# Other scratch tiles for the quadrant sums, and an earlier place for the next layer's value weights, in a two-layer encoder kernel

## The chip, the cores and the metric

The kernel runs on one core of a Trainium2 chip. The metric is the device time of one execution in microseconds (us), given as the median of several runs. The engines are called as in the profile: PE (TensorE, with PEld for its weight loads), DVE (VectorE), ACT (ScalarE), POOL (GpSimd) and SP (SyncE, whose queue issues all the DMAs here). Each engine runs its own instructions in the order in which they stand in the program.

## The reference

Two layers over 512 tokens of width 1024, in float32. What matters here is the end of a layer and the start of the next one:

```
for l in range(2):
    proj = x @ w_in[l]                       # 1024 x 6816; columns 1024..1535 are the values of neighbourhood attention
    ... three attentions, gates, merge ...
    x = layer_norm(ALPHA * x + merged @ w_out[l])
    gu = x @ w_ffn_in[l]                     # 1024 x 5632
    hidden = silu(gu[:, :2816]) * gu[:, 2816:]
    x = layer_norm(ALPHA * x + hidden @ w_ffn_out[l])
```

## The kernel before, in words

Every float32 operand is split into a high and a low part (`split`, `wsplit`: ACT copies the high part with a rounding, L138 or L221; DVE subtracts it for the low part, L139 or L222), and each product is three matmuls (high x high, high x low, low x high). `x` is kept transposed as `xth` and `xtl`. A scheduler fixes the order of the instructions on every engine when the program is built; the order of the code, the buffers of the pools and the slots decide what it may move.

**Feed-forward.** The 2816 hidden columns are 11 sets of 256. `CHUNKS` groups the sets in four chunks of 3, 3, 3 and 2. The first set of a layer is `ffn_plain`. The others are `ffn_fast`, a Strassen-like scheme on quadrants of `x` (two halves of the 1024 rows by two halves of the tokens) with seven products instead of eight. PE's seven products (L778) go into three PSUM tiles: `px` and `pz` (both of tag `sc`) and `py` (tag `pv`). `py` takes three products one after the other (sum t2, sum t3, sum t4), and DVE reads it between them (L844, L848, L857), so that the next product waits for that read. Two buffers each serve `sc` and `pv`.

**The quadrant sums.** The sums of quadrants of `x` (t1 to t4) are made once in each layer, in its first fast set, by `x_sums` (L731 to L760): for each of two halves nine DVE adds and subtractions of 128x512, and four splits (four ACT copies L221, four DVE subtractions L222). Its three scratch tiles come from the pool tag `P` (`ptile`, four buffers). The same four buffers hold the plain set's two `hidden` tiles (`sg`, L784 and L785) and the fast set's `p1`. The 16 slots of the sums stay taken until after the last set.

**Slots.** `R` is a first-in first-out list of 38 tiles of 128x512 (names r0_74 and so on in the rows). The list is worked through while the program is built, so the place of a `put` in the code decides which tiles the next `get` receives.

**The down products.** `ffn_down` loads weights of `w_ffn_out` in pieces of 512 KB into the two `raw` buffers, splits them, and adds each token tile's product to `xt` on DVE (L878). The down product of a chunk is put behind the first two sets of the next chunk, one half of the columns behind each. The last chunk's down product stands at the end of the layer. Ahead of it, in layer 0, `wload_slots` loads the value weights of layer 1 (four pieces of 512 KB through the same two `raw` buffers) and splits them into 16 slots of `R`. A `raw` buffer is free for its next load when both halves of the piece in it have been split.

Of the kernel before, what the change touches and what calls it, by code (L numbers as in the profile page):

```python
# [9 lines left out]
F32 = mybir.dt.float32  # L10
# [8 lines left out]
DEPTH = 2  # L19
D_IN = 6816  # L20
D_FF = 2816
# [5 lines left out]
C_NQ, C_NK, C_NV = 0, 512, 1024  # L27
# [54 lines left out]
def trunk(ctx, tc, x, ln_in, w_in, feat, bias, lamv, w_mla, w_mlr, w_mlv, w_branch, w_out,  # L82
# [36 lines left out]
    def ptile():  # L119
        return dp.tile([128, 512], F32, tag="P", name="P", bufs=4)  # L120
# [76 lines left out]
    def wload_slots(src_of, ncol, steps):  # L197

        res, slots, k = [], [], 0
        for n in steps:  # L200
            raw = wp.tile([128, 1024], F32, tag="raw", name="raw", bufs=2)
            rv = raw[:, :n * ncol].rearrange("p (k c) -> p k c", k=n)
            c = 0
            for src in src_of(k * 128, (k + n) * 128):
                w = src.shape[1]
                nc.sync.dma_start(rv[:, :, c:c + w], src.rearrange("(k p) c -> p k c", p=128))
                c += w
            hl = ([], [])
            for a in range(0, n * ncol, 512):
                hi, lo = R.get(), R.get()  # L210
                split(hi, lo, raw[:, a:a + 512])
                hl[0].append(hi)
                hl[1].append(lo)
            slots += hl[0] + hl[1]
            res.append((k, n, tuple(Pairs(i, ncol) for i in hl)))
            k += n
        return res, slots
# [66 lines left out]
    na_v, na_slots = [], []  # L284
# [447 lines left out]
    def x_sums():  # L732

        h = lambda kh, th: f32(quad(xth, kh, th))
        lo = lambda kh, th: f32(quad(xtl, kh, th))
        two = lambda t: t.rearrange("p (k c) -> p k c", k=2)
        res = [[], [], [], []]
        for i in range(2):
            ts = [ptile() for _ in range(3)]
            t1, t2, d = (two(t) for t in ts)  # L740
            q = lambda a: a[:, 2 * i:2 * i + 2]

            def halves(n, t):
                hl = (R.get(), R.get())
                split(*hl, t)
                res[n].append(hl)

            V.tensor_sub(t1, q(h(0, 1)), q(h(0, 0)))
            V.tensor_sub(d, q(lo(0, 1)), q(lo(0, 0)))
            V.tensor_add(t1, t1, d)  # L750
            V.tensor_sub(t2, q(h(1, 1)), t1)
            V.tensor_add(t2, t2, q(lo(1, 1)))
            halves(1, ts[1])
            halves(0, ts[0])
            V.tensor_sub(d, t2, q(h(0, 0)))
            V.tensor_sub(d, d, q(lo(0, 0)))
            halves(2, ts[2])
            V.tensor_sub(t1, q(h(1, 0)), t2)
            V.tensor_add(t1, t1, q(lo(1, 0)))
            halves(3, ts[0])  # L760
        return res
# [51 lines left out]
    def ffn_fast(l, m, sums):  # L813


        early = not sums

        def load(t, base, kh):
            c = slice(base + m * 128, base + (m + 2) * 128)
            nc.sync.dma_start(t.rearrange("p (k c) -> p k c", k=4),  # L820
                              w_ffn_in[l, kh * 512:(kh + 1) * 512, c].rearrange("(k p) c -> p k c", p=128))
            return t

        def halved(t, now=True):
            return wsplit(t, 1024, now)

        g0, u0, u1 = load(H.get(), 0, 0), load(H.get(), D_FF, 0), load(H.get(), D_FF, 1)
        s = H.get()
        g1 = load(wp.tile([128, 1024], F32, tag="raw", name="raw", bufs=2), 0, 1)
        px, py, pz = bank("sc"), bank("pv"), bank("sc")  # L830
        product(px, halved(g0, not early), from_x(0, 0), True)
        p1 = ptile()
        A.activation(p1, px, AF.Copy)  # L833
        if early:
            product(px, halved(g1, False), from_x(1, 0), False)
            sums += x_sums()
        t1, t2, t3, t4 = sums
        with tc.high_priority():
            V.tensor_add(s, u0, u1)
            V.tensor_sub(u0, g0, u0)  # L840
            V.tensor_sub(g0, s, g0)
        product(py, halved(g0), from_sum(t2), True)
        u2 = ptile()
        V.tensor_add(u2, py, p1)  # L844
        product(pz, halved(s), from_sum(t1), True)
        product(py, halved(u0), from_sum(t3), False)
        u3 = ptile()
        V.tensor_add(u3, py, p1)  # L848
        V.tensor_add(u3, pz, u3)
        if not early:  # L850
            product(px, halved(g1), from_x(1, 0), False)
        with tc.high_priority():
            V.tensor_sub(g1, g1, g0)
        product(pz, halved(g1), from_x(1, 1), False)
        V.tensor_add(u2, pz, u2)
        product(py, halved(u1), from_sum(t4), False)
        V.tensor_add(p1, py, p1)  # L857
        H.put(s, u0, g0, u1)
        res = [hidden(px, p1)]
        res.append(hidden(u2, u3))  # L860
        return res

    def ffn_down(l, m0, sets, xt, first, hfs):

        n = 2 * len(sets)
        act = tuple(HidTiles(sets, i) for i in range(2))
        chs = []
        for hf in hfs:
            c = slice(hf * 512, (hf + 1) * 512)
            chs.append((c, wload_ks(lambda a, e: [w_ffn_out[l, m0 * 128 + a:m0 * 128 + e, c]], 512, (2,) * (n // 2))))  # L870
        for t in range(NT):
            for c, ch in chs:
                p = bank("acc")
                gemm_x(p, ch, slice(0, 512), act, tsl(t), n)
                if first:
                    V.scalar_tensor_tensor(xt[t][:, c], xt[t][:, c], ALPHA, p, op0=OP.mult, op1=OP.add)
                else:
                    V.tensor_add(xt[t][:, c], xt[t][:, c], p)  # L878
            yield t
        if 1 in hfs:  # L880
            for st in sets:
                for hl in st:
                    R.put(*hl)


    for l in range(DEPTH):
# [87 lines left out]
        for c, (m0, n) in enumerate(CHUNKS):  # L974
            sets = []
            for i in range(n):
                m = 2 * (m0 + i)
                if m0 + i == 0:
                    sets.append(ffn_plain(*plain[0]))
                else:  # L980
                    sets.append(ffn_fast(l, m, sums))
                if done is not None and i < 2:
                    for _ in ffn_down(l, *done, xt, c == 1, (i,)):
                        pass
            done = 2 * m0, sets
        for t in sums:
            for hl in t:
                R.put(*hl)
        gb = load_gb(ln2[l])
        if l < DEPTH - 1:  # L990
            na_v, na_slots = wload_slots(lambda a, e: [w_in[l + 1, a:e, C_NV:C_NV + 512]], 512, (2, 2, 2, 2))
        for t in ffn_down(l, *done, xt, False, (0, 1)):
            layer_norm(xt[t], *gb)
            if l == DEPTH - 1:
# [93 lines left out]
```

## Time and profile before

| | |
|---|---|
| median of 3 runs | 1885.93 us (1885.37 to 1889.29) |
| the profiled execution's own time | 1881.28 us |
| its span, first to last instruction | 1879.3 us |
| PE busy | 1822.4 us, 97% of the span |
| DVE busy | 1331.0 us, 71% |
| ACT busy | 906.0 us, 48% |
| mean granted TensorE clock | 0.990 |

The span is what the trace covers, and the execution's own time is 2 us longer. PE leaves 57 us of the span idle. A matmul that is issued late, or that runs at the half clock, counts as busy for longer, so the busy share alone does not tell what could be saved.

### The profile page before, as it was taken

How to read it: one execution, taken by the hardware profiler on the slowest of the kernel's cores; microseconds unless marked ns; L12 is line 12 of the kernel's file. 1: busy time of each engine (PE TensorE's matmuls, PEld its weight loads, DVE VectorE, ACT ScalarE, POOL GpSimd, SP SyncE). 2: the span in 40 equal slices, each digit the busy share in tenths (PEclk: the TensorE clock that was granted, in tenths of full speed). 3: DMA queues.
4: the chain of work that ended last, by engine and by line, in shares of the span. 5: the costliest groups of instructions: out<-in, count | busy, mean ns of one | idle time of the engine just before them, and what ended most of it. 6: DMA issues, size and time to landing. Idle time of an engine off the chain costs nothing.

```text
span 1879.3 us, 28551 instructions
## 1 busy us (share of the span) xinstructions
PE 1822.4 (97%) x11200; PEld 1623.1 (86%) x11200; DVE 1331.0 (71%) x2228; ACT 906.0 (48%) x1620; POOL 87.8 (5%) x165
## 2 busy tenths in 40 slices
PE   7999999999998899999899999999999979999998
PEld 6988899988878899999689888999888779899996
DVE  6488886666567877777556888866656678777766
ACT  3567776555423443333326677755554234343431
POOL 4100000000000000000001000000000000000001
PEclk9999999999999899999999999999999999999999
DMA  7453232223251232323345432322233412323332
GB/s 256 120 156 101 89 87 77 79 79 96 90 191 46 68 113 86 117 87 105 126 132 150 127 96 86 91 62 85 74 107 122 147 57 68 115 92 114 96 102 78
DMA packets 167765, 195.86 MB, mean 104 GB/s; under 512 B 8528, under 2 KB 132688, under 8 KB 167632
## 3 DMA queue, kind: packets, MB, share of 16 engines
q1 hardware_dynamic: 167632, 194.05, 33.1%
q8 instruction: 88, 1.44, 0.3%
q14 instruction: 45, 0.37, 0.1%
HBM read 177.24 MB, written 9.44 MB: 99 GB/s over the span
## 4 chain that ended last, share of the span: by engine, by line
PE 89%; DVE 5%; DMA 3%; ACT 2%; issue 1%; SPq 0%; POOLq 0%; DVEq 0%; POOL 0%; ACTq 0%
PE acc L156 18%; PE acc L157 18%; PE acc L158 18%; PE sc L778 10%; PE pv L778 8%; DVE wlo L139 2%; PE tr L648 2%; PE pv L491 1%; DMA raw<-in_w_ffn_in_dram 1%; PE pv L656 1%; PE pv L655 1%; PE sc L477 1%; PE sc L632 1%; PE sc L631 1%; PE sc L476 1%
## 5 line engine op out<-in xcount | busy, mean ns | idle before, releaser
L139 DVE TENSOR_TENSOR wlo<-raw,whi 128x1024 fp32r<-128x1024 f32 (+4 forms) x242 | 287.9, 1191 | 127.1 <-ACT whi L138 124.1
L138 ACT ACTIVATE whi<-raw 128x1024 fp32r<-128x1024 f32 (+4 forms) x242 | 249.9, 1033 | 253.3 <-PE acc L157 49.4
L138 ACT ACTIVATE whi<-f 128x1024 fp32r<-128x1024 f32 x100 | 104.6, 1056 | 214.2 <-PE acc L158 118.8
L156 PE MATMUL acc<-whi,r 128*128 128x512 f32 (+1 forms) x504 | 195.6, 394 | 9.7 <-ACT whi L138 6.1
L156 PE MATMUL acc<-xth,whi 128*128 128x512 f32 x512 | 204.0, 398 | 0.6 <-ACT f L672 0.6
L158 PE MATMUL acc<-xth,wlo 128*128 128x512 f32 x512 | 202.7, 396 | 0.0
L157 PE MATMUL acc<-xtl,whi 128*128 128x512 f32 x512 | 202.6, 396 | 0.0
L157 PE MATMUL acc<-wlo,r 128*128 128x512 f32 (+1 forms) x504 | 198.5, 394 | 1.1 <-DVE wlo L139 1.1
L158 PE MATMUL acc<-whi,r 128*128 128x512 f32 (+1 forms) x504 | 197.7, 392 | 0.0
L778 PE MATMUL pv<-r,whi 128*128 128x256 f32 x960 | 176.0, 282 | 8.8 <-DVE P L844 3.1
L156 PE MATMUL acc<-whi,xth 128*128 128x256 f32 (+2 forms) x544 | 161.8, 299 | 1.6 <-ACT whi L138 1.6
L157 PE MATMUL acc<-wlo,xth 128*128 128x256 f32 (+2 forms) x544 | 162.4, 299 | 0.8 <-DVE wlo L139 0.8
L158 PE MATMUL acc<-whi,xtl 128*128 128x256 f32 (+2 forms) x544 | 162.4, 299 | 0.0
L778 PEld LDWEIGHTS pv<-r,whi 128*128 128x128 f32 x960 | 148.6, 189 | 12.1 <-DVE P L844 3.5
L139 DVE TENSOR_TENSOR wlo<-f,whi 128x1024 fp32r<-128x1024 f32 x100 | 121.5, 1221 | 29.7 <-ACT whi L138 25.8
L778 PE MATMUL sc<-xth,whi 128*128 128x256 f32 x480 | 134.3, 280 | 3.9 <-ACT P L833 3.9
L778 PE MATMUL pv<-r,wlo 128*128 128x256 f32 x480 | 134.7, 281 | 0.0
L778 PE MATMUL sc<-xtl,whi 128*128 128x256 f32 x480 | 133.8, 279 | 0.0
L778 PE MATMUL sc<-xth,wlo 128*128 128x256 f32 x480 | 133.5, 279 | 0.0
L156 PEld LDWEIGHTS acc<-whi,r 128*128 128x128 f32 x504 | 94.8, 190 | 32.3 <-ACT whi L138 6.8
L157 PEld LDWEIGHTS acc<-wlo,r 128*128 128x128 f32 x504 | 95.4, 189 | 23.0 <-DVE wlo L139 2.7
L158 PEld LDWEIGHTS acc<-whi,r 128*128 128x128 f32 x504 | 95.7, 190 | 21.1
(231 smaller groups left out, 4296.1 us busy)
## 6 DMA issues: line engine op xcount, KB each, us to landing
raw<-in_w_in_dram SPq DMA_DIRECT2D x64, 512.0 KB, 3.6
f<-in_w_ffn_in_dram SPq DMA_DIRECT2D x60, 512.0 KB, 3.5
raw<-in_w_ffn_out_dram SPq DMA_DIRECT2D x44, 512.0 KB, 3.6
raw<-in_w_in_dram SPq DMA_DIRECT2D x64, 256.0 KB, 3.3
raw<-in_w_ffn_in_dram SPq DMA_DIRECT2D x28, 512.0 KB, 3.6
raw<-in_w_branch_dram SPq DMA_DIRECT2D x24, 512.0 KB, 3.4
raw<-in_w_out_dram SPq DMA_DIRECT2D x16, 512.0 KB, 3.6
r<-r SPq DMA_DIRECT2D x56, 128.0 KB, 2.5
```

Of the source, the lines that this page charges most:

```text
L138: A.activation(hi[:, :n], raw[:, :n], AF.Copy)
L139: V.tensor_sub(lo[:, :n], raw[:, :n], f32(hi[:, :n]))
L156: T.matmul(o, lh[0], rh[0], start=first, stop=False)
L157: T.matmul(o, lh[0], rh[1], start=False, stop=False)
L158: T.matmul(o, lh[1], rh[0], start=False, stop=last)
L476: T.matmul(sc, qs[j][:, tsl(t)], ks[j][0], start=True, stop=False)
L477: T.matmul(sc, qs[j][:, tsl(t)], ks[j][1], start=False, stop=True)
L491: T.matmul(po[:, 0:256], ch_[:, tsl(k)], v, start=k == 0, stop=False)
L631: T.matmul(sc, q[0][:, tsl(t)], k[0], start=True, stop=False)
L632: T.matmul(sc, q[0][:, tsl(t)], k[1], start=False, stop=False)
L648: T.transpose(pt[:, tsl(i)], prs[i % 2][:, tsl(kp + i // 2)], ident)
L778: T.matmul(o[:, c], w[a][:, j, f], x[e], start=fresh and mi == 0 and j == 0 and n == 0, stop=j == 3 and n == 2, skip_group_check=True)
```

## The change

Three edits. In `x_sums` the three scratch tiles are no longer three of the four `P` tiles: two are taken from the gates' tag `gt` (two buffers) and one from the tag `o32` (one buffer, here named `xs`), both of which the attention phase used before. The sums' slots are returned to `R` right behind the last set, ahead of the down product that follows it. And the value weights of layer 1 are loaded while that down product (the third chunk's second half) is built, behind its first token tile, instead of after it.

```diff
--- before.py
+++ after.py
@@ -736,7 +736,7 @@
         two = lambda t: t.rearrange("p (k c) -> p k c", k=2)
         res = [[], [], [], []]
         for i in range(2):
-            ts = [ptile() for _ in range(3)]
+            ts = gate_tiles() + [dp.tile([128, 512], F32, tag="o32", name="xs", bufs=1)]
             t1, t2, d = (two(t) for t in ts)
             q = lambda a: a[:, 2 * i:2 * i + 2]
 
@@ -979,16 +979,18 @@
                     sets.append(ffn_plain(*plain[0]))
                 else:
                     sets.append(ffn_fast(l, m, sums))
+                last = m0 + i == D_FF // 256 - 1
+                if last:
+                    for t in sums:
+                        for hl in t:
+                            R.put(*hl)
                 if done is not None and i < 2:
-                    for _ in ffn_down(l, *done, xt, c == 1, (i,)):
-                        pass
+                    for t in ffn_down(l, *done, xt, c == 1, (i,)):
+                        if last and t == 0 and l < DEPTH - 1:
+                            na_v, na_slots = wload_slots(lambda a, e: [w_in[l + 1, a:e, C_NV:C_NV + 512]],
+                                                         512, (2, 2, 2, 2))
             done = 2 * m0, sets
-        for t in sums:
-            for hl in t:
-                R.put(*hl)
         gb = load_gb(ln2[l])
-        if l < DEPTH - 1:
-            na_v, na_slots = wload_slots(lambda a, e: [w_in[l + 1, a:e, C_NV:C_NV + 512]], 512, (2, 2, 2, 2))
         for t in ffn_down(l, *done, xt, False, (0, 1)):
             layer_norm(xt[t], *gb)
             if l == DEPTH - 1:
```

What this does to the order on three engines follows. **DVE, layer 0, where the plain set ends and the first fast set starts, before** (xth and xtl are the transposed `x`, f tiles hold raw weights, P_5813 and P_5914 are the plain set's two `sg`, L748 to L759 are the sums' adds):

```order
L841 TENSOR_TENSOR f1_113<-f2_114,f1_113 128x1024
L222 TENSOR_TENSOR xtl_73<-tr_5706,xth_72 128x4x128
L853 TENSOR_TENSOR raw_5922<-raw_5922,f1_113 128x1024
L139 TENSOR_TENSOR wlo_6029<-f1_113,whi_6028 128x1024
L785 TENSOR_TENSOR P_5813<-P_5813,pv_5715 128x512
L139 TENSOR_TENSOR wlo_6059<-f2_114,whi_6058 128x1024
L222 TENSOR_TENSOR r3_77<-P_5813,r2_76 128x512
L785 TENSOR_TENSOR P_5914<-P_5914,pv_5716 128x512
L222 TENSOR_TENSOR r31_105<-P_5914,r30_104 128x512
L748 TENSOR_TENSOR P_5985<-xth_72 128x512
L749 TENSOR_TENSOR P_5987<-xtl_73 128x512
L139 TENSOR_TENSOR wlo_6087<-f0_112,whi_6086 128x1024
```

**The same twelve places after the change:**

```order
L748 TENSOR_TENSOR gt_5985<-xth_72 128x512
L841 TENSOR_TENSOR f1_113<-f2_114,f1_113 128x1024
L222 TENSOR_TENSOR xtl_73<-tr_5706,xth_72 128x4x128
L749 TENSOR_TENSOR xs_5987<-xtl_73 128x512
L853 TENSOR_TENSOR raw_5922<-raw_5922,f1_113 128x1024
L785 TENSOR_TENSOR P_5813<-P_5813,pv_5715 128x512
L139 TENSOR_TENSOR wlo_6029<-f1_113,whi_6028 128x1024
L750 TENSOR_TENSOR gt_5985<-gt_5985,xs_5987 128x512
L139 TENSOR_TENSOR wlo_6059<-f2_114,whi_6058 128x1024
L222 TENSOR_TENSOR r3_77<-P_5813,r2_76 128x512
L751 TENSOR_TENSOR gt_5986<-xth_72,gt_5985 128x512
L222 TENSOR_TENSOR r20_94<-gt_5985,r12_86 128x512
```

All nine adds of the first half, two of its splits and the second half's first add (twelve instructions) now stand ahead of L785 on P_5914, the multiplication that waits for the plain set's last product and that comes eight rows behind the ones shown; before, all of them stood behind it. In layer 1 the same rows move in the same way.

**PE, layer 0, the first fast set, before** (pv_5925 is `py`; w..6086 are the weights of the product with t3, w..6147 those with t4, and w..6194 those of the next set's first product):

```order
L778 MATMUL pv_5925<-r23_97,whi_6086 128x256
L778 MATMUL pv_5925<-r5_79,whi_6086 128x256
L778 MATMUL pv_5925<-r23_97,wlo_6087 128x256
L778 MATMUL sc_6191<-xth_72,whi_6194 128x256
L778 MATMUL sc_6191<-xtl_73,whi_6194 128x256
L778 MATMUL sc_6191<-xth_72,wlo_6195 128x256
L778 MATMUL sc_6191<-xth_72,whi_6194 128x256
```

**After:**

```order
L778 MATMUL pv_5925<-r23_97,whi_6086 128x256
L778 MATMUL pv_5925<-r5_79,whi_6086 128x256
L778 MATMUL pv_5925<-r23_97,wlo_6087 128x256
L778 MATMUL pv_5925<-r14_88,whi_6147 128x256
L778 MATMUL pv_5925<-r16_90,whi_6147 128x256
L778 MATMUL pv_5925<-r14_88,wlo_6148 128x256
L778 MATMUL pv_5925<-r14_88,whi_6147 128x256
```

Before, 23 matmuls of the next set's first product stood between the product with t3 and that with t4; now the product with t4 follows at once, and the next set's product stands behind the first set's last one.

**DVE at the end of layer 0, before** (raw_8819, 8825, 8831 and 8837 are the four pieces of the value weights, acc_8737 to acc_8797 the four token tiles of the third chunk's down product, raw_8843 and the following ones the weights of the last down product, lam1 a scalar of layer 1):

```order
L222 TENSOR_TENSOR r6_80<-raw_8825,r8_82 128x512
L902 TENSOR_TENSOR lam1_9084<-ring_126 128x1
L878 TENSOR_TENSOR f3_115<-f3_115,acc_8737 128x512
L903 TENSOR_SCALAR lam1_9084<-lam1_9084 128x1
L878 TENSOR_TENSOR f5_117<-f5_117,acc_8757 128x512
L222 TENSOR_TENSOR r28_102<-raw_8831,r0_74 128x512
L878 TENSOR_TENSOR f6_118<-f6_118,acc_8777 128x512
L222 TENSOR_TENSOR r25_99<-raw_8825,r27_101 128x512
L222 TENSOR_TENSOR r7_81<-raw_8831,r9_83 128x512
L878 TENSOR_TENSOR f4_116<-f4_116,acc_8797 128x512
L222 TENSOR_TENSOR r29_103<-raw_8837,r1_75 128x512
L222 TENSOR_TENSOR r20_94<-raw_8837,r12_86 128x512
```

**After** (raw_8757, 8763, 8769 and 8775 are now the pieces of the value weights):

```order
L222 TENSOR_TENSOR r21_95<-raw_8763,r13_87 128x512
L222 TENSOR_TENSOR r11_85<-raw_8763,r10_84 128x512
L222 TENSOR_TENSOR r35_109<-P_8714,r33_107 128x512
L878 TENSOR_TENSOR f3_115<-f3_115,acc_8737 128x512
L898 SCALAR_TENSOR_TENSOR P_9075,ring_126<-P_9075 128x64 x2
L222 TENSOR_TENSOR r24_98<-raw_8769,r26_100 128x512
L222 TENSOR_TENSOR r4_78<-raw_8769,r22_96 128x512
L878 TENSOR_TENSOR f5_117<-f5_117,acc_8781 128x512
L902 TENSOR_TENSOR lam1_9084<-ring_126 128x1
L222 TENSOR_TENSOR r5_79<-raw_8775,r23_97 128x512
L903 TENSOR_SCALAR lam1_9084<-lam1_9084 128x1
L222 TENSOR_TENSOR r16_90<-raw_8775,r14_88 128x512
```

The splits of the value weights now write other slots (the former sums' r13, r10, r26, r22, r23, r14 in place of r8, r0, r27, r9, r1 of the third chunk's hidden tiles), and all stand ahead of the third token tile's addition, which is the row behind these; the second and third L878 each stand behind a split of a piece that was loaded late. On SP one row moves: the third piece's load stands ahead of the load of layer 1's lambda vectors instead of behind it. Beyond these places, the orders are the same up to the names of slots.

## Rows read from the trace of the kernel before

**Rows 1.** The page, part 1: busy us, share of the span and instructions.

```profile
PE 1822.4 (97%) x11200; PEld 1623.1 (86%) x11200; DVE 1331.0 (71%) x2228; ACT 906.0 (48%) x1620; POOL 87.8 (5%) x165
```

**Rows 2.** Stretches: length, busy per engine (instructions), PEclk, DMA share, GB/s.

```profile
599.74:636.25 36.51, 26.67 (x195) 25.28 (x194) 30.85 (x41) 13.84 (x19) 0.00 (x0) 0.86 0.09 29
612.00:618.00 6.00, 2.29 (x9) 1.93 (x9) 5.90 (x10) 1.71 (x3) 0.00 (x0) 0.50 0.15 53
1534.10:1569.55 35.45, 26.75 (x195) 25.36 (x194) 29.66 (x41) 12.76 (x18) 0.00 (x0) 0.86 0.10 31
915.95:942.59 26.64, 20.04 (x73) 14.89 (x73) 17.63 (x25) 5.38 (x6) 2.50 (x4) 0.87 0.46 155
```

**Rows 3.** Timeline of DVE, layer 0: start, us, line, operation, idle before and its releaser.

```profile
583.27 1.23 DVE L839 TENSOR_TENSOR f<-f,f 128x1024 f32<-128x1024 f32 x1 [2.41 <-DMA f<-in_w_ffn_in_dram]
...
592.01 0.68 DVE L222 TENSOR_TENSOR r<-P,r 128x512 fp32r<-128x512 f32 x1
...
600.01 0.69 DVE L785 TENSOR_TENSOR P<-P,pv 128x512 f32<-128x512 f32 x1 [7.31 <-PE pv L158]
...
602.00 0.69 DVE L748 TENSOR_TENSOR P<-xth 128x512 f32<-128x512 f32 x1
...
603.69 1.22 DVE L139 TENSOR_TENSOR wlo<-f,whi 128x1024 fp32r<-128x1024 f32 x1 [0.40 <-ACT whi L138]
...
620.14 1.29 DVE L222 TENSOR_TENSOR r<-P,r 128x512 fp32r<-128x512 f32 x2
```

**Rows 4.** Timeline of PE, layer 0, the first fast sets.

```profile
604.20 0.39 PE L778 MATMUL sc<-xth,whi 128*128 128x256 f32 x1 [1.58 <-ACT P L833]
...
608.91 0.38 PE L778 MATMUL pv<-r,whi 128*128 128x256 f32 x1 [0.90 <-ACT r L221]
...
610.63 0.58 PE L778 MATMUL pv<-r,whi 128*128 128x256 f32 x1 [1.34 <-DVE r L222]
...
615.63 1.31 PE L778 MATMUL sc<-r,whi 128*128 128x256 f32 x2 [3.56 <-ACT r L221]
...
624.83 0.50 PE L778 MATMUL pv<-r,whi 128*128 128x256 f32 x2 [2.31 <-DVE P L844]
...
636.25 0.40 PE L778 MATMUL pv<-r,whi 128*128 128x256 f32 x2
...
645.74 0.40 PE L778 MATMUL pv<-r,whi 128*128 128x256 f32 x2
...
648.57 0.28 PE L778 MATMUL sc<-xth,whi 128*128 128x256 f32 x1
```

**Rows 5.** The page, part 6: loads by size, median us from issue to landing.

```profile
raw<-in_w_in_dram SPq DMA_DIRECT2D x64, 512.0 KB, 3.6
```

**Rows 6.** Timeline of ACT at the end of layer 0.

```profile
899.29 0.63 ACT L221 ACTIVATE r<-raw 128x512 fp32r<-128x512 f32 x1 [0.86 <-DMA raw<-in_w_in_dram]
...
912.96 0.63 ACT L221 ACTIVATE r<-raw 128x512 fp32r<-128x512 f32 x1 [5.39 <-PE acc L157]
...
917.92 1.15 ACT L221 ACTIVATE r<-raw 128x512 fp32r<-128x512 f32 x2 [2.93 <-DMA raw<-in_w_in_dram]
...
920.38 1.06 ACT L138 ACTIVATE whi<-raw 128x1024 fp32r<-128x1024 f32 x1 [1.31 <-DMA raw<-in_w_ffn_out_dram]
```

**Rows 7.** Timeline of SP's DMA queue at the end of layer 0: start, us until the last was issued.

```profile
894.70 5.61 SPq L206 DMA_DIRECT2D raw<-in_w_in_dram  x2
...
903.43 11.28 SPq L206 DMA_DIRECT2D raw<-in_w_in_dram  x2
...
915.74 10.52 SPq L129 DMA_DIRECT2D raw<-in_w_ffn_out_dram  x4
```

**Rows 8.** Timeline of PE at the end of layer 0, the two down products.

```profile
907.29 0.51 PE L156 MATMUL acc<-whi,r 128*128 128x512 f32 x1 [0.84 <-DVE lam L903]
...
921.49 0.80 PE L156 MATMUL acc<-whi,r 128*128 128x512 f32 x1 [5.54 <-ACT whi L138]
...
928.72 0.50 PE L157 MATMUL acc<-wlo,r 128*128 128x512 f32 x1 [0.35 <-DVE wlo L139]
```

## The prediction, made before the changed kernel ran

> **What bounds the kernel now.** I read the page's first part, then the waits of PE, then stretches of the places that the change touches, and last the timelines of each engine there. PE is busy for 97% of the span [rows 1], so it is the bound nearly everywhere, and a change helps only where PE stands still or runs slowly. Three such places lie where the change acts.
>
> The first two are the first fast set of each layer. I cut the stretch from the start of that set's first product to the start of the product with w6227 (192 matmuls of 128x256). It takes 36.51 us in layer 0 and 35.45 us in layer 1 [rows 2]. At full speed 24 such matmuls take 2.83 us (645.74 to 648.57 in [rows 4]), so 192 need 22.7. The excess, 13.8 and 12.8 us, has two parts. PE waits: 1.58, 0.90, 1.34, 3.56 and 2.31 us, 9.7 in all, mostly for the quadrant sums' splits, the last for L844 [rows 4]. And the granted clock is 0.86 over the stretch, 0.50 from 612 to 618 [rows 2]: the lower of its two levels, 1.2 GHz, after the waits had come close together. DVE tells why the sums are late. It works without a break once the adds begin at 602.00 and ends the last split at 621.4 (620.14 and 1.29), and just before, it stood still for 7.31 us in front of L785, which waited for the plain set's last product [rows 3]. The sums need only `xth` and `xtl`, which DVE had finished before 592.01 [rows 3].
>
> The third place is the end of layer 0. PE ends the third chunk's down product at 915.95 and waits 5.54 us for the last down product's first weights, then three short ones behind it (the last, 0.35, in [rows 8]). From 915.95 to 942.59 the clock is 0.87 [rows 2]. The chain backward: that weight piece's load was issued at 915.74 [rows 7] and split from 920.38 [rows 6]. It waited for a `raw` buffer, the buffer for a split of value weights, and that split stood still for 5.39 us until 912.96 for PE's L157 on acc [rows 6]: it writes a slot that the third chunk's down product was still reading.
>
> **The change part by part.** No instruction is added or removed; the sum is all in order and waits. Durations: a DVE operation of 512 columns 0.69 us, followed by the next after 0.60; the low split of 1024 columns 1.22, next after 1.13 [rows 3]; an ACT copy of 512 0.63, of 1024 1.06 [rows 6].
>
> *Scratch tiles, DVE.* Twelve instructions of the sums move ahead of that L785. From L839 at 583.27 [rows 3] I walk the new order. L748 starts at 586.3; the first half's adds, in between the set's other work, run until 599.5; L748 of the second half ends 600.2, and L785 starts when PE lets it, at 600.0 or 600.2. Twelve times 0.61 is 7.3 us, all in the hole of 7.31. The rest follows in order and the last split ends at 613.6, 7.8 us earlier than 621.4.
>
> *Scratch tiles, PE, layer 0.* Same walk. The first 24 matmuls end at 602.5, the two groups of 6 on the first half's sums run straight on to 603.9 (they waited before). ACT now splits the t3 weights, then copies `px` (L833) by 604.2: wait 0.3. 24 matmuls to 607.05, 18 on t1 to 609.2; on t2 one matmul, then a wait of 1.4 for the low part of the second half's t2 sum (DVE, 610.7); 17 to 612.75. The product with t3 needs L844, which stands behind the sums' end (613.6) and L839: 615.4, a wait of 2.6. 24 to 618.2. The product with t4 follows at once in the new order, without the 23 matmuls that filled this place; L848 stands behind a low split, L840 and L841 (3 x 1.15) and ends at 619.5: wait 1.3. Then 72 matmuls without a wait to 628.1. Waits 5.6 instead of 9.7. Each restart costs about 0.1 more (the first matmul after a wait shows 0.38 to 0.39 against 0.28 [rows 4]). 22.7 + 5.6 + 0.4 = 28.7 us against 36.51: 7.8 less, at the full clock. Does the clock fall again? Before, it was low by 612, after waits of 1.58, 0.90 and 1.34; 1.4 and 2.6 in a row may do the same, and 24 matmuls at half clock cost 2.83 more, of which the wait for L848 hides 1.3 (1.5 net), some more if it lasts. Bounds 0 and 2.2; I take 1.1. Layer 0: 7.8 - 1.1 = **6.7** (5.6 to 7.8). Layer 1 has the same order 934.36 us later: 35.45 - 28.7 - 1.1 = **5.6** (4.6 to 6.7).
>
> For the clock there is a rule in the Trainium skill, "TensorE: Matmul & The Clock Gate" (section "What's actually happening"): the slow clock is the default, and activity releases it. The trace agrees as far as 0.50 after close waits goes; by this rule the waits left over would keep the clock low as long as before, and the sum would lose the 1.1 us in each layer.
>
> *Slots and value weights.* The new slots are those of the sums, last read by the last set's products, which PE had left behind before 907.29 [rows 8]. So the wait of 5.39 goes, and what is late next is a load's landing. From issue to landing takes 3.6 us by the median [rows 5]; 894.70 to 899.29 is 4.6 [rows 6, 7], under other loads. With 3.6: the second piece is issued by 900.3 as before [rows 7] and split by 905.5. The third goes out at 901.75, when the first piece's second split is done (before: 903.43), and frees its buffer at 908.8, behind the two L898. The fourth goes out at 905.5 instead of 914.3 (903.43 and 11.28 to the end of its issue [rows 7]), and its last split ends at 911.2. So the first weights of the last down product go out at 908.8 instead of 915.74, and are split by 914.7, before PE asks at about 915.4. The second piece goes out at 911.2 and its low part is ready at 917.1, the third at 914.7 and 920.6, the fourth at 917.1 and 923.0. PE (0.233 us each, six matmuls 1.4) takes piece 1 to 916.8, waits some 0.1 and takes piece 2 to 918.4, waits 1.0 for piece 3's high part and 1.0 for its low part: its second matmul on piece 3 starts at 920.65, which is the one at 928.72 in [rows 8]. 8.1 us less, half clock included. With 4.6 for each landing the three loads in that chain add 3: 5.1 less. The median is nearer; I take **7.3**.
>
> What is queued behind the new waits: the third chunk's additions (L878) stand behind splits of pieces still to land. The first now ends at about 906.8; PE's third token tile waited for it until 907.29 [rows 8], so nothing is lost. The second ends at 909.4 and is needed at 911; the third at 912.0, needed at 915.4. A landing 1.6 us late in the third piece begins to cost PE.
>
> The earlier load of the third piece puts the lambda load behind it by 0.1 us, hidden behind the same issue. The slots that neighbourhood attention takes next were released earlier or as before, since both orders hand out the same number: nothing.
>
> For the load, "SBUF — State Buffer" in the Trainium skill (section "The DMA setup-cost knee") fits a fixed 2 us and 436 GB/s: an estimate of 3.2 us for 512 KB. The rows show 3.6 and more, so they decide; by the page the chain of three would gain 1.2 more.
>
> **Sum.** 6.7 + 5.6 + 7.3 = 19.6 us. PE is busy without such waits behind each place, so it stays saved. The own time, 1881.28, becomes 1861.7. The median of the runs is 4.65 above the profiled execution; 1885.93 - 19.6 = 1866.3, and I say **1866.5 us**.
>
> **Rivals.**
> - *The waits only move.* DVE is busy 30.85 of 36.51 us in that stretch [rows 2], so it nearly sets its length; the waits left are L844 and L848 with nothing in between, and if the half clock stays, the loads take 4.6 and each of the two reads comes 1 us later, I get 7.8 - 2.2 - 2 = 3.6 in layer 0, 2.5 in layer 1 and 5.1 at the end of layer 0, 11.2 us in all: 1874.7. For it: the t4 product's lost filler. Against it: DVE starts 7.3 us sooner whatever PE does.
> - *The sums gain nothing.* If L748 had to wait for something else, or L785 were held, only the 7.3 us at the end of layer 0 would be left: 1878.6. The order and the dependences speak against it.
> - *No change.* What is saved is lost to the loads of the next sets, which then come too late. Against it: the next sets' weights are loaded into buffers that are freed earlier too. 1884 to 1888.
> - *Slower.* At the end of layer 0 the additions L878 are held behind splits of loads. If pieces land so late that the third token tile waits, PE loses each microsecond beyond a margin of 1.6. To turn the sum over by 4 us, it takes some 25 us of lateness there, or the four loads landing in 10 us each; the slowest in the rows took 4.6. 1890 or more.
>
> **How the numbers follow.** Chances: the forecast 0.68, waits that move 0.20, no gain in the sums 0.05, no change 0.04, slower 0.03. The likeliest gives 1866.5. Above, the range goes to 1876, which takes in the second case; below, it goes to 1860.5, with the upper bounds 7.8, 6.7 and 8.1 (22.6 in all) and no wait for L848 in either layer (2.6 more). The likeliest case alone spans 1863.3 (22.6 less) to 1870.6 (the lower bounds 5.6, 4.6 and 5.1). A difference of 0.2% (3.8 us) is about what a measurement can tell. Faster 0.93, within 0.2% 0.04, slower 0.03.
>
> **What the changed profile would show.** Right: L748 on DVE at about 586 in layer 0, no idle of 7 us before L785, and the last split of the sums about 14 us after the first fast product starts instead of 21.7; PE's longest waits in that stretch before L844's and L848's readers; and ACT's splits of the value weights no longer waiting for PE, with PE's wait of 5.54 us down to some 1 us. Wrong: a clock of 0.5 for longer than 8 us in either layer, or PE waiting for L878 between the token tiles. The prediction fails by most if the saved time comes back as a wait further on, which the stretch lengths of the later sets would show.

## The result, and the profile after

The changed kernel takes 1861.88 us (median of 4 runs, 1859.15 to 1864.11) where the kernel before took 1885.93 in the runs beside it (1885.37 to 1889.29): a ratio of 0.9868, 95% interval 0.9851 to 0.9886. It is faster by 24 us; 1866.5 was forecast, with a range of 1860.5 to 1876, so the time lies near the lower end of it. The profiled execution's own time is 1861.61 us, 19.7 less than before's 1881.28; the forecast for it was 1861.7.

First the page's part 1 of the changed kernel, against [rows 1]:

```profile
PE 1814.6 (98%) x11200; PEld 1617.4 (87%) x11200; DVE 1331.0 (72%) x2228; ACT 905.3 (49%) x1620; POOL 88.2 (5%) x165
```

The instructions are the same in number. PE is busy for 7.8 us less with the same work: the page counts a matmul at the half clock for longer (in the trace before, a matmul of 128x512 is counted with 0.63 us between 921.49 and 927, where the granted clock is 0.50, and with 0.39 elsewhere).

Then the stretches that answer to [rows 2], with the same columns: the first fast set of layer 0 and of layer 1 up to the same 192 matmuls, six microseconds of layer 1 and the first two of them alone, and the last down product's start at the end of layer 0.

```profile
605.50:634.00 28.50, 23.52 (x194) 22.71 (x193) 26.57 (x35) 12.98 (x17) 0.00 (x0) 1.00 0.18 54
1521.17:1550.96 29.79, 24.78 (x195) 23.89 (x193) 26.40 (x34) 12.45 (x16) 0.00 (x0) 0.94 0.18 52
1539.00:1545.00 6.00, 5.22 (x35) 4.92 (x34) 4.20 (x5) 1.54 (x2) 0.00 (x0) 0.74 0.00 0
1539.00:1541.00 2.00, 2.00 (x12) 2.00 (x11) 1.68 (x2) 0.00 (x0) 0.00 (x0) 0.50 0.00 0
911.00:931.05 20.05, 18.49 (x78) 13.98 (x77) 15.21 (x23) 3.18 (x3) 2.49 (x4) 1.00 0.40 131
```

28.50 us instead of 36.51, and 29.79 instead of 35.45. In layer 0 the granted clock is 1.00 all through; in layer 1 it fell once: it is 0.50, the lower of its two levels, from 1539 to 1541, and 0.74 is the mean from 1539 to 1545. At the end of layer 0 it is 1.00 where it was 0.87.

The timeline of DVE in layer 0, against [rows 3]:

```profile
592.20 0.68 DVE L748 TENSOR_TENSOR gt<-xth 128x512 f32<-128x512 f32 x1
...
604.68 0.69 DVE L759 TENSOR_TENSOR gt<-gt,xtl 128x512 f32<-128x512 f32 x1
605.28 0.68 DVE L748 TENSOR_TENSOR gt<-xth 128x512 f32<-128x512 f32 x1
605.88 0.68 DVE L785 TENSOR_TENSOR P<-P,pv 128x512 f32<-128x512 f32 x1
...
618.82 0.68 DVE L222 TENSOR_TENSOR r<-gt,r 128x512 fp32r<-128x512 f32 x1
...
620.56 0.68 DVE L844 TENSOR_TENSOR P<-pv,P 128x512 f32<-128x512 f32 x1
...
624.68 0.68 DVE L848 TENSOR_TENSOR P<-pv,P 128x512 f32<-128x512 f32 x1
```

The sums begin at 592.20, ahead of the second L785, which now follows without any idle time (no bracket at 605.88; before, 7.31 us). The last split ends at 619.50, 14.0 us after the first fast product's start; before, 21.7.

PE over the same stretch, against [rows 4]:

```profile
605.50 0.28 PE L778 MATMUL sc<-xth,whi 128*128 128x256 f32 x1
...
609.97 0.39 PE L778 MATMUL sc<-xth,whi 128*128 128x256 f32 x1 [0.22 <-ACT P L833]
...
616.62 0.39 PE L778 MATMUL pv<-r,whi 128*128 128x256 f32 x1 [1.32 <-DVE r L222]
...
621.29 0.50 PE L778 MATMUL pv<-r,whi 128*128 128x256 f32 x2 [2.40 <-DVE P L844]
...
625.42 0.51 PE L778 MATMUL pv<-r,whi 128*128 128x256 f32 x2 [1.04 <-DVE P L848]
...
634.00 0.40 PE L778 MATMUL pv<-r,whi 128*128 128x256 f32 x2
```

Four waits are left, 4.98 us together instead of 9.7. The longest, 2.40, and the one of 1.04 stand in front of products that share the bank `pv` and wait for DVE's reads L844 and L848; the one of 1.32 waits for a split of the sums (L222).

The end of layer 0: ACT's splits (against [rows 6]), SP's queue (against [rows 7]) and PE (against [rows 8]).

```profile
902.90 1.15 ACT L221 ACTIVATE r<-raw 128x512 fp32r<-128x512 f32 x2 [1.05 <-DMA raw<-in_w_in_dram]
...
905.76 1.16 ACT L221 ACTIVATE r<-raw 128x512 fp32r<-128x512 f32 x2 [0.19 <-DMA raw<-in_w_in_dram]
908.86 1.06 ACT L138 ACTIVATE whi<-raw 128x1024 fp32r<-128x1024 f32 x1 [1.94 <-DMA raw<-in_w_ffn_out_dram]
```

```profile
891.39 7.41 SPq L206 DMA_DIRECT2D raw<-in_w_in_dram  x3
...
902.16 0.37 SPq L206 DMA_DIRECT2D raw<-in_w_in_dram  x1
904.88 9.45 SPq L129 DMA_DIRECT2D raw<-in_w_ffn_out_dram  x4
```

```profile
903.38 0.50 PE L156 MATMUL acc<-whi,r 128*128 128x512 f32 x1 [0.26 <-DVE f L878]
...
913.99 0.50 PE L157 MATMUL acc<-wlo,r 128*128 128x512 f32 x1 [0.31 <-DVE wlo L139]
...
915.92 0.50 PE L156 MATMUL acc<-whi,r 128*128 128x512 f32 x1 [0.49 <-ACT whi L138]
917.18 0.50 PE L157 MATMUL acc<-wlo,r 128*128 128x512 f32 x1 [0.76 <-DVE wlo L139]
```

No split of the value weights waits for PE any more; each waits for its load. The first weights of the last down product are issued 10.3 us after the third chunk's down product starts (904.88, 894.56), where it took 17.9 before (915.74 in [rows 7], 897.88), and PE reaches them without a stop: its first wait behind 903.38 is the one at 913.99, for a low part.

**Where the time went.** The two profiled executions, the changed one less the one before, at the same instruction: the first fast product of layer 0 starts 5.76 us later (605.50, 599.74), and the end of that stretch comes 2.25 earlier; the third chunk's down product starts 3.32 earlier (894.56, 897.88), the second matmul on the third piece behind it 11.54 earlier (917.18, 928.72); the first fast set of layer 1 starts 12.93 earlier and its stretch ends 18.59 earlier (1550.96, 1569.55); the end comes 19.7 earlier. So the three places gave 8.0, 8.2 and 5.7 us, 21.9 in all, the stretches between them another 3.6, and 5.76 were lost ahead of the first place, in work whose instructions and order are the same in both kernels.

That loss belongs to the execution, not to the change: in the profiled executions of the ten experiments below, the first fast product starts between 602.27 and 604.40, with scratch tiles moved or not; the profiled execution before (599.74) was the earliest of all, the changed one (605.50) the latest. The first difference lies at the very start, where PE's first wait is 9.66 us in the execution before and 10.7 to 11.5 in the other eleven. The loss is enough to explain why the two traces differ by 19.7 only where the medians differ by 24.05.

### The profile page after: what moved, and what is told of

The parts are those of the page before. It is cut to its first block, busy times and chain, and to the rows that moved or that the text cites. A ratio compares the mean times of both kernels' runs of the same rounds, so it can differ in the third digit from the quotient of the medians.

```text
span 1859.6 us, 28547 instructions
## 1 busy us (share of the span) xinstructions
PE 1814.6 (98%) x11200; PEld 1617.4 (87%) x11200; DVE 1331.0 (72%) x2228; ACT 905.3 (49%) x1620; POOL 88.2 (5%) x165
## 4 chain that ended last, share of the span: by engine, by line
PE 89%; DVE 4%; DMA 3%; ACT 2%; issue 1%; POOL 1%; POOLq 0%; SPq 0%; DVEq 0%; ACTq 0%
PE acc L156 18%; PE acc L157 18%; PE acc L158 18%; PE sc L778 11%; PE pv L778 8%; PE tr L648 2%; DVE wlo L139 1%; PE pv L491 1%; DMA raw<-in_w_ffn_in_dram 1%; ACT whi L138 1%; PE pv L656 1%; PE pv L655 1%; PE sc L477 1%; PE sc L632 1%; PE sc L631 1%
## 5 line engine op out<-in xcount | busy, mean ns | idle before, releaser
L778 PE MATMUL pv<-r,whi 128*128 128x256 f32 x960 | 175.8, 282 | 9.9 <-DVE P L844 4.8
L778 PEld LDWEIGHTS pv<-r,whi 128*128 128x128 f32 x960 | 148.2, 189 | 13.4 <-DVE P L844 5.2
L778 PE MATMUL pv<-r,wlo 128*128 128x256 f32 x480 | 134.7, 281 | 0.0
L778 PE MATMUL sc<-xth,whi 128*128 128x256 f32 x480 | 133.9, 280 | 0.7 <-ACT P L833 0.7
L778 PE MATMUL sc<-xtl,whi 128*128 128x256 f32 x480 | 133.7, 279 | 0.0
L778 PE MATMUL sc<-xth,wlo 128*128 128x256 f32 x480 | 133.3, 279 | 0.0
```

What stands on the lines that cost most here:

```text
L778: T.matmul(o[:, c], w[a][:, j, f], x[e], start=fresh and mi == 0 and j == 0 and n == 0, stop=j == 3 and n == 2, skip_group_check=True)
```

## The experiments

They ran in three groups, each beside the kernel before, whose median was 1884.36 us in the first group (9 runs; with the two single edits, the held sums and the first run of the own banks), 1883.1 in the second (29 runs; with the third tile, the first two tiles and the own banks twice) and 1883.92 in the third (17 runs; with the hidden tiles and `p1` elsewhere). Gains are against its median in the same group.

**One edit at a time.** Only the scratch tiles:

```diff
-            ts = [ptile() for _ in range(3)]
+            ts = gate_tiles() + [dp.tile([128, 512], F32, tag="o32", name="xs", bufs=1)]
```

> The kernel before with the first edit alone (the sums' scratch tiles from gt and o32). Theory: the sums' adds start in DVE's idle time before L785 in both layers, so this gives the part forecast for the two first fast sets, 12.3 us by the forecast and about 15 us by the trace of the changed kernel (stretch of 192 products 28.5 us in layer 0, about 30 in layer 1, instead of 36.5 and 35.5; some small waits behind them gone too): ratio 0.992 to 0.9935. Rival A, the tiles free the P buffers for the sets in general and the later sets gain: the 192-product stretches stay above 33 us and the gain lies behind them. Rival B, most of the gain is at the end of layer 0: ratio above 0.997.

Measured: 1869.21 us, ratio 0.9917 (0.9904 to 0.9931), 15.2 us less. The stretches take 28.9 and 29.7 us, much as in the changed kernel (28.5 and 29.8):

```profile
603.00:631.88 28.88, 23.53 (x194) 22.72 (x193) 27.24 (x37) 13.90 (x18) 0.00 (x0) 1.00 0.18 55
1527.82:1557.54 29.72, 24.99 (x194) 24.18 (x193) 26.39 (x34) 12.45 (x16) 0.00 (x0) 0.94 0.17 53
```

At the end of layer 0 nothing changed; its PE row there is that of [rows 8] once more:

```profile
915.84 0.79 PE L156 MATMUL acc<-whi,r 128*128 128x512 f32 x1 [5.71 <-ACT whi L138]
```

Only the slots (the loop that returns the sums' slots stands behind the last set, the value weights are loaded where they were):

```diff
...
+                if last:
+                    for t in sums:
+                        for hl in t:
+                            R.put(*hl)
...
```

> The kernel before with the second edit alone: the sums' slots are returned behind the last set, and the value weights are still loaded where they were in the code, behind the third chunk's down product. Theory: what held the splits were the slots, not the place of the load; the scheduler puts the loads in the same order either way, so this alone gives the whole gain at the end of layer 0: the ACT wait for PE of 5.39 us is gone, PE's wait of 5.54 us too, 8 us in all, ratio 0.9950 to 0.9965. Rival: the load's place in the code gives the gain; then this one shows a ratio of 0.998 or more and PE still waits over 3 us before the last down product.

Measured: 1876.82 us, ratio 0.9959 (0.9946 to 0.9971), 7.5 us less. Here the stretch in layer 0 is 36.5 us as before, with DVE's hole, and at the end of layer 0 the splits wait for loads and not for PE. The two rows are DVE's and ACT's:

```profile
602.54 0.69 DVE L785 TENSOR_TENSOR P<-P,pv 128x512 f32<-128x512 f32 x1 [7.10 <-PE pv L158]
```

```profile
908.97 1.15 ACT L221 ACTIVATE r<-raw 128x512 fp32r<-128x512 f32 x2 [1.28 <-DMA raw<-in_w_in_dram]
```

The two parts add up: 15.2 + 7.5 = 22.7 us against 24.05 for all three edits, whose interval goes from 21.5 to 28.1 us. The third edit has nothing left to do: in the trace of the kernel with the slots alone, where the value weights' load stands at its old place in the code, the order of the instructions of ACT, DVE and SP at the end of layer 0 is already that of the changed kernel. The first and third edits without the second, and the first two without the third, were not run; without the early return the list has only 2 of its 38 slots free at that place (16 hold the sums, 20 the hidden tiles of five sets), and the value weights need 16.

**Is it the start of the sums, or the tiles as such?** The changed kernel with one column of the plain set's second hidden tile copied into t1 ahead of the sums, so that t1's adds cannot start before that tile is done; the column is overwritten by the add:

```diff
...
+            if i == 0:
+                V.tensor_copy(ts[0][:, 0:1], f32(after[:, 0:1]))
...
```

> The changed kernel with one instruction more: a copy of one column of the plain set's second hidden tile into the first scratch tile, ahead of the sums, so that the sums' own scratch tiles stay but their adds (all but one) can't start before the plain set's last product is multiplied. The column is overwritten, nothing else changes. Theory: the gain in the first fast sets is DVE's idle time filled, so it goes: 192-product stretches back to 35 to 37 us, DVE idle about 7 us before L785, and only the 8 us at the end of layer 0 stay: ratio 0.995 to 0.997. Rival, own buffers as such help (nothing waits for a P tile): the ratio stays below 0.992.

Measured: 1872.84 us, ratio 0.9943 (0.993 to 0.9957), a little better than the 0.995 to 0.997 expected, and far from the rival's 0.992 or less. The hole in front of the second multiplication (L787 here) is back, and with it PE's long wait for a split of the sums (L780 is L778 here):

```profile
603.54 0.69 DVE L787 TENSOR_TENSOR P<-P,pv 128x512 f32<-128x512 f32 x1 [8.13 <-PE pv L158]
```

```profile
618.37 0.58 PE L780 MATMUL sc<-r,whi 128*128 128x256 f32 x1 [5.28 <-ACT r L221]
```

The stretches are not quite back to the 35 to 37 us expected:

```profile
603.27:637.71 34.44, 25.22 (x194) 24.11 (x193) 29.05 (x41) 12.59 (x18) 0.00 (x0) 0.90 0.10 31
1524.91:1559.36 34.45, 25.21 (x194) 24.11 (x193) 29.04 (x41) 12.71 (x18) 0.00 (x0) 0.90 0.10 32
```

They are 2.1 and 1.0 us shorter than before, which with the 8.2 of the end of layer 0 makes 11.3 of the 11.5 us gained. So some 3 us of what the scratch edit gives come without the early start; the rest, 7.6 + 5.7 in the kernel with that edit alone less these 3, needs it. Where the 3 us come from is not shown, but they do not need all three tiles: the two kernels that follow, which move one tile or two and leave the sums late, have stretches of about the same length.

**Which tile held the sums?** The prediction did not ask. My theory was that the plain set's hidden tiles held the buffers of `P` which t1 and t2 wanted. Two kernels move part of the scratch only, on the kernel before:

```diff
-            ts = [ptile() for _ in range(3)]
+            ts = [ptile() for _ in range(2)] + [dp.tile([128, 512], F32, tag="o32", name="xs", bufs=1)]
```

> The kernel before with one edit: only the third scratch tile of the sums is taken from the tag o32, the first two stay in P. Theory that the sums were held because their first tiles had to wait for a buffer of P that the plain set's second hidden tile still filled: the adds still stand behind that tile's multiplication, so the idle of some 7 us on DVE ahead of L785 and the stretch of 36.5 us in layer 0 stay; ratio to before 0.998 to 1.002. Rival, that one tile more is enough, since the four P buffers then serve four tiles at a time: as with the scratch edit alone, 0.990 to 0.994.

```diff
-            ts = [ptile() for _ in range(3)]
+            ts = gate_tiles() + [ptile()]
```

> The kernel before with the first two scratch tiles taken from gt and the third left in P. Theory that the first two tiles are what held the sums: the first half's adds stand ahead of L785 as with all three tiles moved, the stretch of 192 products takes 28.5 to 30 us in each layer, ratio to before 0.990 to 0.994 (with all three: 0.9917). Rival, that the third tile is then the one that waits for P: the adds that read it stop behind the multiplication, the stretch takes 33 to 35 us, 0.996 to 0.999.

Measured: 0.9989 (0.9979 to 0.9998) for the third tile alone, 0.9987 (0.9978 to 0.9997) for the first two: 1881.72 and 1881.43 us. The first is as expected in its ratio and in DVE's idle time ahead of L785 (8.14 us), but not in its stretches, which take 34.0 and 34.9 us where 36.5 was expected for layer 0: the 3 us of the held sums again. The second misses: the theory asked for 0.990 to 0.994, and it falls; its rival, 0.996 to 0.999 with stretches of 33 to 35 us, is what came (34.1 and 34.8). DVE in that kernel:

```profile
591.40 0.68 DVE L748 TENSOR_TENSOR gt<-xth 128x512 f32<-128x512 f32 x1
...
604.67 0.69 DVE L785 TENSOR_TENSOR P<-P,pv 128x512 f32<-128x512 f32 x1 [6.25 <-PE pv L158]
606.05 0.69 DVE L222 TENSOR_TENSOR r<-P,r 128x512 fp32r<-128x512 f32 x1 [0.70 <-ACT r L221]
606.66 1.28 DVE L749 TENSOR_TENSOR P<-xtl 128x512 f32<-128x512 f32 x2
```

The add into t1 runs early, but L749, into the third tile, stands behind the hidden tile's split, and everything else needs it. Whichever tile is left in `P` is late. What stands between them in the code is `p1`, which L833 fills only when the first fast product is done. Two more kernels part the two suspects: the hidden tiles in `gt`, or `p1` in `o32`, with the sums left in `P`. With the hidden tiles in `gt`, the four buffers of `P` are enough for `p1` and the first half's three scratch tiles, so that kernel also tells whether buffers were simply short.

```diff
+        sg = gate_tiles()
...
-            res.append(hidden(pg[h], pu[h]))
+            res.append(hidden(pg[h], pu[h], sg[h]))
```

> The kernel before with the plain set's two hidden tiles taken from gt and the sums left in P. Theory that p1 is what held the sums: buffers of P are handed out in the order of the code, p1 stands ahead of the sums there and is first written by L833, behind the first fast product; so nothing is gained, DVE's idle of some 7 us ahead of L785 stays and the ratio to before is 0.997 to 1.001. Rival, that the plain set's hidden tiles held the buffers: the adds move ahead of L785, 0.990 to 0.994.

```diff
-        p1 = ptile()
+        p1 = dp.tile([128, 512], F32, tag="o32", name="xs", bufs=1) if early else ptile()
```

> The kernel before with only p1 of the first fast set taken from the tag o32; the sums stay in P. Theory that p1 held them: the first half's adds start right behind the split of the first hidden tile, ahead of the second L785, ten instructions of 0.6 us fill the idle of 7.3 us but for 1 us, the stretch of 192 products takes 29 to 31 us in each layer, ratio to before 0.9915 to 0.9945. Rival, that the hidden tiles held them: nothing moves, 0.998 to 1.001.

Measured: the hidden tiles elsewhere 1883.73 us, 0.9996 (0.9986 to 1.0006), nothing gained; `p1` elsewhere 1869.13 us, 0.9923 (0.9906 to 0.994), within the noise as good as moving all three scratch tiles (0.9917), with stretches of 29.1 and 29.5 us. DVE with the hidden tiles moved, ACT there (L834 is the copy L833), and DVE with `p1` moved:

```profile
603.36 0.69 DVE L785 TENSOR_TENSOR gt<-gt,pv 128x512 f32<-128x512 f32 x1 [6.55 <-PE pv L158]
...
605.35 0.68 DVE L748 TENSOR_TENSOR P<-xth 128x512 f32<-128x512 f32 x1
```

```profile
606.92 0.58 ACT L834 ACTIVATE P<-sc 128x512 f32<-128x512 f32 x1
```

```profile
595.45 0.69 DVE L748 TENSOR_TENSOR P<-xth 128x512 f32<-128x512 f32 x1
...
602.50 0.69 DVE L785 TENSOR_TENSOR P<-P,pv 128x512 f32<-128x512 f32 x1 [0.51 <-PE pv L158]
```

So `p1` held the sums, by its place in the tag and not by its data: with the hidden tiles moved, L748 starts at 605.35, before `p1` is written at 606.92, so on the chip it waits for no reader or writer of `p1`. It is late because the program was built with it behind L785, and it was so built wherever a scratch tile of the sums came after `p1` in the same tag (the kernel before, the third tile alone, the first two tiles, the hidden tiles elsewhere), and not where none did (all three moved, `p1` moved). The expectation's reason, that buffers of a tag are handed out in the order of the code, fits all of them; no run shows it by itself.

**The waits that are left.** In the changed kernel the first fast set waits longest for L844, and for L848 too, since three products share `py`. Here the products with t3 and t4 get banks of their own in the first fast set (one copy of 128x512 on DVE more in each layer):

```diff
-        product(py, halved(u0), from_sum(t3), False)
+        y3, y4 = (bank("acc"), bank("tr")) if early else (py, py)
+        product(y3, halved(u0), from_sum(t3), early)
...
-        V.tensor_add(u3, py, p1)
+        V.tensor_add(u3, y3, u2 if early else p1)
+        if early:
+            V.tensor_copy(p1, u3)
...
-        product(py, halved(u1), from_sum(t4), False)
-        V.tensor_add(p1, py, p1)
+        product(y4, halved(u1), from_sum(t4), early)
+        V.tensor_add(p1, y4, p1)
```

On the changed kernel, twice, and on the kernel before:

> The changed kernel; in each layer's first fast set the products with t3 and t4 go into PSUM banks of their own (tags acc and tr, idle there) instead of on top of the t2 product, and DVE adds them up (one copy of 128x512 more per layer). Theory: the waits left in that set are PE waiting for DVE's reads of py (2.40 and 1.04 us in layer 0, 2.40 and 0.78 in layer 1, and the half clock after them in layer 1); these go, the stretch of 192 products falls to 25 or 26 us in both layers, and the time is 6 to 8 us below the changed kernel: ratio to before 0.982 to 0.985. Rival, DVE sets the length of the stretch anyway (it is busy for 27 of 28.7 us): the waits come back at the next product that needs a sum or a split, and the time is that of the changed kernel, ratio 0.986 to 0.988.

> The changed kernel with the banks of their own, once more beside the same edit on the kernel before: 0.981 to 0.984 as the first time (0.9823).

> The kernel before with the banks of their own for the products with t3 and t4 in the first fast set, and nothing else of the change. Theory that the two limits stand one behind the other (first the late sums, then the reads L844 and L848 of the bank that three products share): with late sums only the wait for L844 (2.31 us in layer 0, 0.78 in layer 1) and what the half clock cost behind it can go, 3 to 5 us in all, ratio to before 0.997 to 0.999. Rival, that the banks give what they give on the changed kernel (1861.88 to 1850.0, 11.9 us): 0.9937.

Measured: on the changed kernel 1850.0 us, ratio to before 0.9823 (0.9808 to 0.9837), and in the second group 1849.55, 0.9818 (0.9803 to 0.9833); on the kernel before 1880.16, 0.9977 (0.9967 to 0.9987). The same edit gives some 10 us behind the change (34.4 and 33.6 us less than before, each in its own group, where the change alone gives 24.05) and 2.9 without it. The 11.9 us of the expectation are the difference of two medians from different groups; the stretches of the two traces are shorter by 4.6 and 6.1, 10.7 together. That is more than the 6 to 8 us expected: the wait of 1.32 us for a split of the sums, which the theory did not name, went as well. The two stretches on the changed kernel, the one wait that is left in layer 0, and the two stretches on the kernel before:

```profile
603.10:627.04 23.94, 22.98 (x195) 22.59 (x193) 23.87 (x33) 12.66 (x17) 0.00 (x0) 1.00 0.14 45
1513.57:1537.26 23.69, 22.67 (x194) 22.10 (x193) 23.15 (x31) 11.63 (x15) 0.00 (x0) 1.00 0.14 46
```

```profile
614.33 0.50 PE L778 MATMUL tr<-r,whi 128*128 128x256 f32 x2 [0.96 <-ACT whi L138]
```

```profile
603.61:637.55 33.94, 27.84 (x195) 26.15 (x193) 31.98 (x44) 14.31 (x19) 0.00 (x0) 0.85 0.10 32
1535.09:1569.18 34.09, 27.88 (x195) 26.20 (x193) 31.69 (x44) 14.19 (x19) 0.00 (x0) 0.85 0.10 32
```

With both, 192 matmuls take 23.9 and 23.7 us, 1.0 to 1.2 above the 22.7 of full speed, and the clock is 1.00 in both layers. DVE is now busy for 23.87 of the 23.94 us in layer 0, so little more can be had there unless DVE gets less work. With late sums the clock is 0.85 and PE still waits for the splits. This version beats both kernels.

## Why the prediction was right, by its steps

- **The waits of the first fast set, layer 0.** Forecast 0.3, 1.4, 2.6 and 1.3 us, measured 0.22, 1.32, 2.40 and 1.04, in the places named and behind the instructions named. The stretch without a loss of clock was put at 28.7 and took 28.50. The sums' last split came 14.0 us after the first product, as forecast. Only the sign named for the profile was put too narrowly: PE's longest waits were to be those for L844 and L848, but the one for the t2 sum's split (1.32) is longer than the one for L848, as the forecast's own 1.4 and 1.3 had it. DVE's work behind 602.00 in [rows 3] was also not quite without a break (0.40 us at 603.69), which changes nothing.
- **The clock.** 1.1 us was set aside in each layer, between bounds of 0 and 2.2. In layer 0 nothing was lost (1.00), so the term is 8.0 and not 6.7; in layer 1 the same four waits (0.50, 1.32, 2.40 and 0.78) were followed by a mean of 0.74 from 1539 to 1545 and a stretch 1.3 us longer, so the term is 5.7 (5.6 forecast). The kernel with the scratch edit alone did the same: 1.00 in layer 0, a mean of 0.87 from 1539 to 1545 and of 0.84 from 1545 to 1551 in layer 1. The Trainium skill's rule, "TensorE: Matmul & The Clock Gate" (section "What's actually happening"), that the slow clock is the default, which activity releases, would have it fall in both layers as I used it; the trace agrees in layer 1 and not in layer 0.
- **The end of layer 0.** 7.3 us forecast (5.1 to 8.1), 8.2 measured. What is late next is the load, as said: the four splits start 0.2 to 1.8 us after ACT is free, all for DMA, and the last piece of the value weights took 3.6 us from its issue to its split (902.16 to 905.76). The chain took 22.6 us from the start of the third chunk's down product to the second matmul on the third piece, 22.8 in the walk with landings of 3.6; it was not the landings that made it so, for the chain's three loads took 4.5, 4.0 and 3.6 us from issue to split (898.43 to 902.90, 904.88 to 908.86, 911.20 to 914.81). What made up for them is that the third piece's buffer was free 6.45 us after that piece's issue and not the 7.05 of the walk. PE's waits at the last down product are 0.31, 0.49 and 0.76 (0.1, 1.0 and 1.0 forecast), and the clock no longer fell there.
- **The additions L878 behind the splits.** This was the way to a slower kernel. PE waited for L878 once, 0.26 us at 903.38, and nowhere else at the end of that layer: the price was named and stayed small.
- **The sum.** 19.6 us against 21.9 at the three places: the clock of layer 0 and the end of layer 0 were mis-sized by 1.3 and 0.9 us, and both came out just past their upper bounds (8.0 against 7.8, 8.2 against 8.1). By the medians the gain is 24.05 us (21.5 to 28.1), 4.4 more than forecast. Besides these 2.3 us, some 2 lie in short waits behind the two first fast sets, a term that the sum put at nothing: from the end of layer 0's stretch to the third chunk's down product PE's waits add up to 0.25 us instead of 1.50, behind layer 1's stretch to 0.26 instead of 1.00. So the median lies 1.4 us below the span of the likeliest case, 1863.3 to 1870.6, and inside the range because its lower end also took in a wait that did not go away (for L848). That the profiled execution came out at 1861.61, almost the 1861.7 forecast for it, is chance, since the 3.6 us gained between the places and the 5.76 lost ahead of them do not stem from the terms. Taking the gain off the median and not off the early profiled execution was right; the gain was too small.
- **The mechanism.** The prediction took the reordering from the built program and was right on its effect, but it spoke of tiles for the sums, and the experiments show that `p1` in the same tag was what kept them late. One tile moved does what three do. The third edit, which the prediction costed together with the second, adds nothing to it.

Of the rivals, that the waits only move (1874.7) is refuted by the stretches; what it named, L844 and L848, is what is left, and the banks show that it was worth some 10 us more. That the sums gain nothing (1878.6) is refuted by the scratch tiles alone, 15.2 us; the slots alone give 7.5, with 7.3 forecast for that part.

## What to carry to other kernels

An engine that stands idle while work without missing inputs lies behind its next instruction has an order problem: look at which tiles of one tag stand ahead of that work in the code, and move the one that is filled late. Limits stand one behind the other: the own banks were worth 2.9 us while the sums were late and some 10 afterwards, so an edit that gave little is worth trying again when the wait ahead of it is gone. And compare two traces place by place, since the totals of two single executions can differ by several microseconds in work that no edit has touched.

## What the runs showed that I had not expected

- Nearly the same four waits in the two layers let the clock fall in layer 1 and not in layer 0, in the changed kernel and in that with the scratch tiles alone. With `p1` elsewhere, where PE waits 1.61 and 1.56 us with one matmul between, it fell in both layers, as these stretches of that kernel show. What tells the layers apart is open.

```profile
614.00:620.00 6.00, 5.32 (x33) 5.11 (x31) 4.42 (x7) 2.86 (x4) 0.00 (x0) 0.72 0.17 60
1538.00:1544.00 6.00, 5.93 (x35) 5.73 (x35) 5.50 (x9) 2.33 (x5) 0.00 (x0) 0.72 0.26 87
```

- Ahead of any edit, the first fast product of layer 0 started between 599.74 and 605.50 us in twelve profiled executions. Part of it is the start (9.66 us to PE's first matmul in one, 10.7 to 11.5 in the others), part lies in the output projection of layer 0, where PE's longest wait for L711 was 0.92 in the execution before and 1.12 to 2.82 in the others.
